# A hybrid mLSTM and sliding-window layer on one core: an account of PSUM banks for the interleaved chains, matrix-memory scores after their exponentials, and an out-projection norm in two operations

## The chip, the cores and the metric

The kernel runs on one core of a Trainium2 chip. The core has a matmul engine (TensorE, in the profile PE, with its weight loads shown apart as PEld), a vector engine (VectorE, DVE), an activation engine (ScalarE, ACT), a general engine (GpSimd, POOL) and an engine that issues most of the DMA transfers (SyncE, SP). Each engine works through its own queue of instructions in order; they wait for each other on semaphores. Matmul results land in PSUM, which this kernel uses as eight banks of 512 fp32 columns; everything else lies in SBUF.

The metric is the device time of one launch in microseconds (us). Lower is better.

## The reference, cut to what matters

One layer of a streaming encoder, on 2048 prompt rows (one sequence) and 128 sample rows (8 sequences of 16 rows with a cached state), each row 1024 wide, all in fp32:

```
z  = x @ w_in                       # q, k, v, output gate (4 heads x 128), two gates per head,
                                    # q (8 x 64), k and v (2 x 64) of the window attention
A: matrix memory, 4 heads, causal:  s = (q k^T) * exp(dmat - mt)
   num = w_inter * (q C) + s v ;  den likewise ;  h = num / max(|den|, exp(-mt))
   C' = decay * C + (wk * k)^T v    # state carried from chunk to chunk
   hm = sigmoid(o) * head_norm(h)
B: window attention: softmax over own and two earlier chunks of 64 rows, with a learned sink;
   mx = max(max(s), sink) ;  p = exp(s - mx) / (sum + exp(sink - mx))
mix = concat(hm, ha) @ w_out
h   = layer_norm(alpha * x + mix)   # the norm of the out-projection: g, b of 1024
u = h @ w_up ; causal conv of width 3 ; silu(gate) * value ; @ w_down
y   = layer_norm(alpha * h + f)
```

The outputs are y, the states of the matrix memory, the last keys and values, and the last rows of the convolution.

## The kernel before, in words

Rows are handled in 17 tiles of 128: 16 of the prompt and one (number 16) of all samples. Large products are made in three fp32r products of a high and a low half (`split` makes the halves: ACT casts, line 207, DVE subtracts, line 208), and many of them by a scheme of seven products for a 2 x 2 block.

The work runs in stages. First the in-projection (`i_dense`): four blocks of four tiles (the first has the sample tile too), and in each block five groups of columns with seven products each, and between blocks the narrow product of gates, keys and values (`i_direct`, `i_keys`). Then the out-projection (`o_block`): blocks of 3, 4, 4, 4 and 2 tiles. Then the up-projection, and then the down-projection.

The two token-mixing parts are chains of small steps, one tile after another: `m_chain` for the matrix memory, `a_chain` for the window attention, `t_sample` for the sample tile. They are written as generators, and their matmuls are placed by hand between those of the in-projection and the out-projection: PE's queue has the order in which the program writes it. The order on the other engines is made by the framework's scheduler.

The class `Chains` decides the place. It keeps a clock of its own, `t`. Each stretch of dense matmuls adds its cost to the clock (645 for 6 matmuls of 256 columns). Each step of a chain yields two numbers: the cost of its matmuls, and how long it then has to wait. `weave` takes the next step of a chain as soon as the clock has passed that time. `until` and `drain` take steps without waiting, where the out-projection needs a tile that is not mixed yet.

A chain's matmuls write to five PSUM banks that they share (`bank`, pool `tps`); the other three hold the dense results. For a tile of the matrix memory, in order: the gate rows are turned (pgr, `gate_rows`, `m_rows`), repeated over partitions (pm), and their columns taken (pcol); then scores (pscore) and turned keys (pkt); then numerators (pnum, two banks) and the state's products (pcu, two banks), from which DVE makes the new state C (line 1195) and `m_norm` the normed rows; then their transposes (pht). For a tile of the window attention: turned queries and keys (pq, pk), twice two banks of scores (psc), transposes of the probabilities (ppt, line 1310), products with the values (ppo).

In `m_tile` the step after pm computes the scores, the turned keys and the exponentials on ACT; the next takes the weighted scores (sd), the weighted keys (kw) on DVE and the weighted queries (qk times wi) on POOL.

The out-projection adds each half of a tile's product to alpha times x (line 1567), and after the second half calls `norm`: statistics on DVE, an inverse root on POOL (line 1524), then ACT (line 1537), DVE (line 1538) and POOL (line 1539), one after another over 1024 columns, and SP stores the row tile to `zh` (line 1570). In the out-projection the mixed rows of the next block are loaded and split too (`x_pair`), half of the low parts on POOL (line 881).

A block's tiles may enter the chains when `i_done` is raised: a counter of items after the narrow products of the block's first two tiles. The logarithms of the gates (`logs_of`, `gate_logs`, ending at line 976) come some items before that.

Of the kernel before, what the change touches and what calls it, by code (L numbers as in the profile page):

```python
# [30 lines left out]
NEG = -1e30  # L31
RING = 3

WB = 4
# [119 lines left out]
class Chains:  # L154

    def __init__(self, p):
        self.t, self.hold = 0.0, False
        self.done = {"m": -1, "a": -1, "s": False}  # L160
        self.p = p
        p.chains = self
        self.live = [[p.t_sample(), 0.0], [p.m_chain(), 0.0], [p.a_chain(), 0.0]]

    def step(self, c):
        r = next(c[0], None)
        if r is None:
            self.live.remove(c)
            return
        self.t += r[0]  # L170
        c[1] = self.t + r[1]

    def weave(self, dense):
        for cost in dense:
            self.t += cost
            if self.hold:
                continue
            for c in list(self.live):
                if c[1] <= self.t:
                    self.step(c)  # L180
# [14 lines left out]
class Prog:  # L195
# [377 lines left out]
    def i_dense(self):  # L573
        nc, a = self.nc, self.a
# [32 lines left out]
        after = None  # L607
        for item in self.items:
            if after:

                after[0] -= 1
                if after[0] == 1:
                    self.logs_of(after[1] - 1)
                if after[0] < 0:
                    self.i_done = after[1]
                    after = None
            self.chains.hold = item[0] == "t" and item[1] > 0
            if item[0] == "t":
# [8 lines left out]
                if ti == 1:  # L627
                    if b + 1 < nb:
                        self.x_steps(b + 1, 1, 2)
                    else:  # L630
                        self.release(4)
                    after = [4, b + 1]
                elif ti == 3 and b or ti == 4:
# [82 lines left out]
    def i_keys(self, b, ti, ps):  # L716
        nc = self.nc
        t = IBLOCKS[b][ti]
        kv = self.mp.tile([P, 2 * P], F32, name="kve", tag="kve", bufs=2)
        nc.scalar.copy(kv, ps[:, 8:264])  # L720
        nc.scalar.copy(self.gates[b][:, ti, :], ps[:, :8])
        self.rope(kv[:, :P], t, 1, nc.vector, self.zev())
        nc.sync.dma_start(self.zkv[t], kv)
# [115 lines left out]

    def rope(self, A, t, nt, adder, B=None):  # L840

        V = self.nc.vector
        n = A.shape[-1]
        if B is None:
            B = self.mp.tile([P, 512], F32, name="rb", tag="rb", bufs=1)
        B = B[:, :n]
        r, i0 = self.angles[t]
# [16 lines left out]
    def zev(self):  # L864
        return self.mp.tile([P, 512], F32, name="zev", tag="zev", bufs=6)

# [43 lines left out]

    def bank(self, shape, name):
        return self.tps.tile(shape, F32, name=name, tag="tb")

    def t_setup(self):
# [12 lines left out]
        self.sinkx = ld("sinkx")  # L927
        self.m0 = ld("m0")
        self.gm = ld("gm")
        nc.vector.tensor_scalar_mul(self.gm, self.gm, 0.5)  # L930
# [93 lines left out]
    def m_chain(self):  # L1024
# [4 lines left out]
        for t in range(NPT):  # L1029
# [3 lines left out]
            if pend is None:  # L1033
                pend = self.m_load(t, b, ti), *self.m_rows(t, b, ti)
                yield 300, 7000
            else:
                yield 0, 1000
            hn = self.m_norm(*(yield from self.m_tile(t, *pend)))
            pend = None
            yield 950, 3000  # L1040
            self.m_scaled(hn)
            if t + 1 < NPT and self.i_done > self.place(t + 1)[0]:
                pend = self.m_load(t + 1, *self.place(t + 1)), *self.m_rows(t + 1, *self.place(t + 1))
            yield 300, 9000
            self.m_out(t, hn[0])
# [114 lines left out]
    def m_tile(self, t, load, i, mp):  # L1160
# [6 lines left out]
        yield 600, 3000  # L1167
        emt = self.m_emt(col)
        ps = self.m_scores(qk)
        kt = self.m_ktok(qk)  # L1170
        wi = self.m_inter(pm, col)
        self.m_exps(dt, col)
        nc.gpsimd.tensor_mul(qk[:, 0:4], qk[:, 0:4], wi)
        yield 950, 6000
        sd = self.m_weighted(ps, dt)
        kw = self.work("kw", [P, MH, P])
        V.tensor_mul(kw, kt, dt[:, :, P - 1:P].to_broadcast([P, MH, P]))
        yield 0, 2500
        num = []
# [63 lines left out]
    def swa(self, t):  # L1243
        nc = self.nc
        V = nc.vector
        if self.a_first is None:
            self.swa_first(t)
            yield 550, 4000
        qh, ql = self.a_first
# [13 lines left out]
        def scores(kvh):  # L1263
            rs = slice(64 * kvh, 64 * kvh + 64)
            sink = self.sink[:, 4 * kvh:4 * kvh + 4]
            sc = self.work("sc", [P, 4, 2 * P], bufs=2)
            mx, es, sm = [self.work(n, [P, 4], bufs=2) for n in ("amx", "aes", "asm")]
            for j0 in (0, 2):
# [3 lines left out]
                for j in range(2):  # L1272
                    V.tensor_tensor_reduce(out=sc[:, j0 + j, :N], in0=ps[:, j, :nk].rearrange("p a b -> p (a b)"), in1=mask, scale=1.0, scalar=-3e38,
                                           op0=ALU.add, op1=ALU.max, accum_out=mx[:, j0 + j:j0 + j + 1])
            V.scalar_tensor_tensor(mx, mx, 0.125, sink, op0=ALU.mult, op1=ALU.max)
            V.tensor_sub(es, sink, mx)
            V.tensor_scalar_mul(mx, mx, -1.0)
            return sc, mx, es, sm
# [11 lines left out]
        z = [scores(0)]  # L1290
        yield 1300, 3000
        exps(*z[0])
# [8 lines left out]
        scs = [x[0] for x in z]  # L1301
        yield 0, 4000

        po = pts = None
        for kt in range(nk + 1):
# [221 lines left out]
    def norm(self, y, g, bb):  # L1527
        for _ in self.norm_steps(y, g, bb):
            pass

# [556 lines left out]
```

## Time and profile before

| | us |
|---|---|
| median of 3 runs | 2447.51 |
| the three runs | 2447.31, 2447.51, 2457.33 |
| the profiled execution, its own time | 2444.13 |
| its span in the profile | 2442.3 |

| stage (us from the start) | what runs |
|---|---|
| 0 to 700 | in-projection, with the sample tile's chain and the prompt tiles' chains 0 to 10 woven in |
| 700 to 960 | out-projection, with the rest of the chains |
| 960 to 2442 | last out-projection blocks, up-projection, down-projection |

The page of the profile gives each engine's busy time as a share of the span (PE 97%, DVE 76%, ACT 51%, POOL 15%), and the granted clock of the matmul engine, 0.988 on average. The list of waits says which instruction waited, for whom, for how long in total, how often and how long at most. The windows give each engine's busy time in a stretch, and the clock in it. A timeline row has the start, the duration, the engine, the line, the operation, what it writes and reads, how many instructions are merged into it and, in brackets, how long the engine was idle before and what ended that.

### The profile page before, as it was taken

To read this page: it belongs to the slowest core of one execution; us is meant where nothing else is said; L and a number is where in the kernel's file an instruction comes from. 1 tells how busy PE (TensorE), PEld (TensorE's weight loads), DVE (VectorE), ACT (ScalarE), POOL (GpSimd) and SP (SyncE) were. 2 spreads that over 40 slices of the span, in tenths; PEclk is the share of its full clock that TensorE was granted. 3 is DMA by queue.
4 is the path that set the end of the run, shared out by engine and by line. 5 is a ranking of instruction groups with operands and counts; after the bars stand their busy time and mean duration, and the time that the engine had idled before them with its cause. 6 is when DMAs were issued, how large, how long until landed. Compare 5 with 4: busy or idle time off the path is not lost.

```text
span 2442.3 us, 39931 instructions
## 1 busy us (share of the span) xinstructions
PE 2357.2 (97%) x14425; PEld 2159.0 (88%) x14425; DVE 1853.2 (76%) x3211; ACT 1252.7 (51%) x2310; POOL 359.1 (15%) x369
## 2 busy tenths in 40 slices
PE   8989999999998899999999999999999999999998
PEld 8989988988987677799999999999999978778776
DVE  8677487686687776997788776778766777896897
ACT  5443365565554553655555555445544544444543
POOL 0101102212224333200000000002000100210400
PEclk9999999999998999999999999999999999999999
DMA  8898988778794446587777889887998776756653
GB/s 292 299 306 308 312 287 300 252 241 298 244 314 150 151 153 230 197 318 289 282 267 269 279 308 324 303 282 243 315 295 260 248 270 212 234 179 216 212 189 104
DMA packets 296933, 624.98 MB, mean 256 GB/s; under 512 B 47004, under 2 KB 140192, under 8 KB 296736
## 3 DMA queue, kind: packets, MB, share of 16 engines
q1 hardware_dynamic: 294144, 612.99, 74.3%
q0 software_dynamic: 1728, 6.29, 0.7%
q10 hardware_dynamic: 864, 3.15, 0.4%
q8 instruction: 114, 1.87, 0.3%
q14 instruction: 83, 0.68, 0.1%
HBM read 451.78 MB, written 170.56 MB: 255 GB/s over the span
## 4 chain that ended last, share of the span: by engine, by line
PE 68%; DVE 11%; DMA 8%; issue 4%; ACT 3%; POOL 1%; SPq 0%; DVEq 0%; ACTq 0%; POOLq 0%
PE fup L1790 15%; PE dps L1790 15%; PE dps L686 10%; PE fht L1993 5%; PE dps L1993 5%; PE fup L1993 3%; DMA zf<-cc 2%; DVE w L208 2%; PE dps L212 2%; PE dps L213 1%; PE dps L214 1%; DVE cc L1838 1%; DVE uw L208 1%; PE ppo L1316 1%; PE ppt L1310 1%
## 5 line engine op out<-in xcount | busy, mean ns | idle before, releaser
L1790 PE MATMUL dps<-hh,uw 128*128 128x384 f32 (+1 forms) x1848 | 481.8, 329 | 8.6 <-ACT u L1815 3.7
L1790 PE MATMUL fup<-hh,uw 128*128 128x384 f32 (+1 forms) x1848 | 481.1, 329 | 3.7 <-ACT u L1815 2.4
L1790 PEld LDWEIGHTS dps<-hh,uw 128*128 128x128 f32 x1848 | 330.2, 188 | 12.4 <-ACT u L1815 4.8
L1838 DVE SCALAR_TENSOR_TENSOR cc<-u,cw,cc 128x768 f32<-128x768 f32 (+1 forms) x264 | 252.5, 978 | 111.3 <-ACT cc L1836 109.3
L1790 PEld LDWEIGHTS fup<-hh,uw 128*128 128x128 f32 x1848 | 330.4, 188 | 5.5 <-ACT u L1815 3.5
L1790 PE MATMUL fup<-hl,uw 128*128 128x384 f32 (+1 forms) x924 | 303.2, 328 | 2.9 <-DVE hl L208 2.9
L1790 PE MATMUL dps<-hl,uw 128*128 128x384 f32 (+1 forms) x924 | 302.8, 328 | 0.0
L686 PE MATMUL dps<-w,oh 128*128 128x256 f32 x1344 | 260.0, 288 | 3.8 <-ACT zev L753 1.4
L208 DVE TENSOR_TENSOR w<-wraw,w 128x1024 fp32r<-128x1024 f32 (+2 forms) x167 | 204.1, 1230 | 68.0 <-ACT w L207 65.8
L207 ACT CAST w<-wraw 128x1024 fp32r<-128x1024 f32 (+2 forms) x167 | 162.8, 983 | 162.0 <-PE dps L686 74.1
L686 PEld LDWEIGHTS dps<-w,oh 128*128 128x128 f32 x1344 | 214.1, 191 | 17.6 <-issue 8.1
L207 ACT CAST uw<-wraw 128x1024 fp32r<-128x1024 f32 x126 | 122.9, 978 | 202.6 <-PE dps L1993 94.1
L208 DVE TENSOR_TENSOR uw<-wraw,uw 128x1024 fp32r<-128x1024 f32 x126 | 150.9, 1199 | 61.7 <-ACT uw L207 61.5
L1836 ACT ACTIVATE cc<-u,cw 128x768 f32<-128x768 f32 (+1 forms) x132 | 129.6, 998 | 124.4 <-DVE u L1829 60.8
L686 PE MATMUL dps<-oh,w 128*128 128x256 f32 x896 | 175.3, 290 | 16.8 <-ACT dps L781 5.9
L686 PE MATMUL dps<-w,ol 128*128 128x256 f32 x672 | 189.7, 282 | 0.0
L1993 PE MATMUL fup<-uw,fu 128*128 128x512 f32 x726 | 176.4, 399 | 8.9 <-DVE yacc L2022 4.5
L1790 PEld LDWEIGHTS fup<-hl,uw 128*128 128x128 f32 x924 | 173.8, 188 | 3.5 <-DVE hl L208 3.5
L1993 PEld LDWEIGHTS fup<-uw,fu 128*128 128x128 f32 x726 | 137.2, 190 | 43.7 <-DVE yacc L2022 5.4
L1790 PEld LDWEIGHTS dps<-hl,uw 128*128 128x128 f32 x924 | 173.8, 188 | 0.0
L686 PEld LDWEIGHTS dps<-oh,w 128*128 128x128 f32 x896 | 145.4, 195 | 25.0 <-ACT dps L781 6.5
L1993 PE MATMUL dps<-uw,fu 128*128 128x512 f32 x660 | 164.7, 396 | 0.0
(331 smaller groups left out, 4818.4 us busy)
## 6 DMA issues: line engine op xcount, KB each, us to landing
uw<-zw SPq DMA_DIRECT2D x176, 512.0 KB, 4.9
zw<-uw SPq DMA_DIRECT2D x88, 512.0 KB, 2.9
w<-zws SPq DMA_DIRECT2D x72, 512.0 KB, 5.6
wv<-wup SPq DMA_DIRECT2D x66, 512.0 KB, 5.2
wraw<-wi SPq DMA_DIRECT2D x65, 512.0 KB, 5.0
wraw<-zt SPq DMA_DIRECT2D x60, 512.0 KB, 4.2
wraw<-wdn SPq DMA_DIRECT2D x45, 512.0 KB, 3.8
wraw<-wo SPq DMA_DIRECT2D x40, 512.0 KB, 4.3
```

The lines of the kernel that those rows point to most:

```text
L207: nc.scalar.copy(hi, src)
L208: nc.vector.tensor_sub(lo, src, hi.bitcast(F32))
L212: mm(out, ah, bh, start=start, stop=False)
L213: mm(out, ah, bl, start=False, stop=False)
L214: mm(out, al, bh, start=False, stop=stop)
L686: mm(o, l, r, start=s in (1, 7) and c == k == i == 0, stop=k == 3 and i == 2, skip_group_check=True)
L1310: nc.tensor.transpose(pp[:, j * P:(j + 1) * P], scs[kvh][:, j, kt * P:(kt + 1) * P], self.ident)
L1316: nc.tensor.matmul(po[64 * kvh:64 * kvh + 64], w, pts[:, kvh], start=kt == 1, stop=kt == nk)
L1790: mm(ps, l[:, k], r[:, k], start=s in (1, 7) and k == 0 and i == 0, stop=k == 3 and i == 2, skip_group_check=True)
L1836: S.activation(c[:, v], u[:, v, 2:2 + n], AF.Identity, bias=w[3], scale=w[2])
L1838: V.scalar_tensor_tensor(c[:, v], u[:, v, i:i + n], w[i], c[:, v], op0=ALU.mult, op1=ALU.add)
L1993: mm(ps, l[:, k, c], r[:, k], start=s in (1, 4, 7) and u == 0 and k == 0 and i == 0, stop=u == nu - 1 and k == n - 1 and i == 2, skip_grou ...
```

## The change

The clock of the chains also keeps a list of five times, one for each bank of the chains' pool. Each call of `bank` drops the oldest entry and appends the present time plus a hold that depends on the bank's name (6500, 4000, 5000, 6500, or 3500 for the others). A step may yield a third number, the banks that the next step will ask for; `weave` takes that step only when so many of the oldest entries have passed.

In `m_tile` the exponentials and the weights `wi` come in a step of their own; scores and turned keys follow 5000 later, together with the weighted scores, keys and queries. Some waiting times of the chains are other numbers.

The norm of the out-projection becomes two DVE operations of full width: (y - mean) * g, and then y * (inverse deviation) + b.

Apart from these: the negated sink is made once, and the negated maximum of the scores comes from one operation and not from two; the counter before `i_done` goes from 4 to 6, the logarithms stay at the same item; evicted keys and values take a slot of the ring `zev` (now seven slots, before six) in place of their own tiles, and their rotation uses the scratch tile `rb`.

```diff
+NBANKS = 5
+HOLDS = {"pm": 6500, "pgr": 4000, "pnum": 5000, "ppo": 6500}
 class Chains:
-        self.live = [[p.t_sample(), 0.0], [p.m_chain(), 0.0], [p.a_chain(), 0.0]]
+        self.live = [[p.t_sample(), 0.0, 0], [p.m_chain(), 0.0, 0], [p.a_chain(), 0.0, 0]]
+        self.free = [0.0] * NBANKS
     def step(self, c):
...
         c[1] = self.t + r[1]
+        c[2] = r[2] if len(r) > 2 else 0
+
+    def ask(self, hold):
+        self.free = self.free[1:] + [self.t + hold]
     def weave(self, dense):
...
-                if c[1] <= self.t:
+                if c[1] <= self.t and max(self.free[:c[2]], default=0) <= self.t:
                     self.step(c)
     def i_dense(self):
...
-                if after[0] == 1:
+                if after[0] == 3:
                     self.logs_of(after[1] - 1)
...
-                    after = [4, b + 1]
+                    after = [6, b + 1]
     def i_keys(self, b, ti, ps):
-        kv = self.mp.tile([P, 2 * P], F32, name="kve", tag="kve", bufs=2)
+        kv = self.zev()[:, :2 * P]
         nc.scalar.copy(kv, ps[:, 8:264])
...
-        self.rope(kv[:, :P], t, 1, nc.vector, self.zev())
+        self.rope(kv[:, :P], t, 1, nc.vector)
     def rope(self, A, t, nt, adder):
-        if B is None:
-            B = self.mp.tile([P, 512], F32, name="rb", tag="rb", bufs=1)
-        B = B[:, :n]
+        B = self.mp.tile([P, 512], F32, name="rb", tag="rb", bufs=1)[:, :n]
     def zev(self):
-        return self.mp.tile([P, 512], F32, name="zev", tag="zev", bufs=6)
+        return self.mp.tile([P, 512], F32, name="zev", tag="zev", bufs=7)
     def bank(self, shape, name):
+        self.chains.ask(HOLDS.get(name, 3500))
         return self.tps.tile(shape, F32, name=name, tag="tb")
     def t_setup(self):
+        self.nsink = self.one("nsink", [P, 8])
+        nc.vector.tensor_scalar_mul(self.nsink, self.sink, -1.0)
     def m_chain(self):
-                yield 300, 7000
+                yield 300, 7000, 2
             else:
-                yield 0, 1000
+                yield 0, 1000, 2
...
-            yield 950, 3000
+            yield 950, 3000, 1
             self.m_scaled(hn)
...
-            yield 300, 9000
+            yield 300, 7500, 1
             self.m_out(t, hn[0])
     def m_tile(self, t, load, i, mp):
         yield 600, 3000
         emt = self.m_emt(col)
+        wi = self.m_inter(pm, col)
+        self.m_exps(dt, col)
+        yield 0, 5000, 2
         ps = self.m_scores(qk)
         kt = self.m_ktok(qk)
-        wi = self.m_inter(pm, col)
-        self.m_exps(dt, col)
-        nc.gpsimd.tensor_mul(qk[:, 0:4], qk[:, 0:4], wi)
-        yield 950, 6000
         sd = self.m_weighted(ps, dt)
         kw = self.work("kw", [P, MH, P])
         V.tensor_mul(kw, kt, dt[:, :, P - 1:P].to_broadcast([P, MH, P]))
-        yield 0, 2500
+        nc.gpsimd.tensor_mul(qk[:, 0:4], qk[:, 0:4], wi)
+        yield 950, 3500, 4
     def a_chain / swa(self, t):
-            yield 550, 4000
+            yield 550, 4000, 2
...
-            V.scalar_tensor_tensor(mx, mx, 0.125, sink, op0=ALU.mult, op1=ALU.max)
-            V.tensor_sub(es, sink, mx)
-            V.tensor_scalar_mul(mx, mx, -1.0)
+            V.scalar_tensor_tensor(mx, mx, -0.125, sink[1], op0=ALU.mult, op1=ALU.min)
+            V.tensor_add(es, sink[0], mx)
...
-        yield 1300, 3000
+        yield 1300, 3000, 2
...
-        yield 0, 4000
+        yield 0, 3500, 2 + 2 * (self.a_load is not None)
...
-            yield (860 if kt < nk else 0) + (1400 if kt else 0), 0 if kt == nk else 1500 if kt else 3000
+            yield (860 if kt < nk else 0) + (1400 if kt else 0), 0 if kt == nk else 1500 if kt else 3000, 2 * (kt + 1 < nk) + (kt == 0)
     def norm(self, y, g, bb):
-        for _ in self.norm_steps(y, g, bb):
-            pass
+        V = self.nc.vector
+        mv, s = self.stats(y)
+        V.scalar_tensor_tensor(y, y, mv[:, 0:1], g, op0=ALU.subtract, op1=ALU.mult)
+        V.scalar_tensor_tensor(y, y, s[:, 0:1], bb, op0=ALU.mult, op1=ALU.add)
```

More of the change, by code (lines that the diff above doesn't have):

```diff
@@ L838, in d_sums, with rope @@
         nc.sync.dma_start(self.zt[1, k], y)
-    def rope(self, A, t, nt, adder, B=None):
+    def rope(self, A, t, nt, adder):
         V = self.nc.vector
         n = A.shape[-1]
-        if B is None:
-            B = self.mp.tile([P, 512], F32, name="rb", tag="rb", bufs=1)
-        B = B[:, :n]
+        B = self.mp.tile([P, 512], F32, name="rb", tag="rb", bufs=1)[:, :n]
         r, i0 = self.angles[t]
@@ L1264, in scores @@
             rs = slice(64 * kvh, 64 * kvh + 64)
-            sink = self.sink[:, 4 * kvh:4 * kvh + 4]
+            sink = [x[:, 4 * kvh:4 * kvh + 4] for x in (self.sink, self.nsink)]
             sc = self.work("sc", [P, 4, 2 * P], bufs=2)
```

## The prediction, made before the changed kernel ran

> **What bounds the kernel now.** I read the page first (busy shares), then the waits of the matmul engine alone, then windows by stage, then the vector and GpSimd timelines around the longest waits.
>
> ```profile
> PE 2357.2 (97%) x14425; PEld 2159.0 (88%) x14425; DVE 1853.2 (76%) x3211; ACT 1252.7 (51%) x2310; POOL 359.1 (15%) x369
> ```
>
> The matmul engine (PE) is busy 97% of the span, and the change leaves the number and shapes of its matmuls as they are (13961 in both written orders). So the change can only win PE's idle time, and the slow stretches that follow it. The waits of PE from 160 to 1000 us, where the chains and the out-projection run (total, times, longest):
>
> ```profile
> PE ppt L1310 <- DVE C L1195: 13.4, 4, 5.1
> PE dps L686 <- ACT dps L781: 6.7, 4, 4.3
> PE dps L686 <- ACT gates L721: 4.8, 4, 2.4
> PE pgr L985 <- DVE g L976: 4.0, 1, 4.0
> PE dps L213 <- DVE w L208: 2.3, 1, 2.3
> PE pm L1079 <- DVE hl L993: 2.1, 1, 2.1
> ...
> PE ppo L1316 <- ACT pth L1311: 1.5, 1, 1.5
> ```
>
> All rows of that answer sum to 40.6 us: the ceiling of idle time. The windows by stage, and short windows just behind four waits (length, PE, PEld, DVE, ACT, POOL busy, granted clock):
>
> ```profile
> 160.00:700.00 540.00, 521.06 (x4144) 484.93 (x4144) 385.28 (x1050) 288.83 (x713) 98.61 (x74) 0.98 0.85 282
> 700.00:960.00 260.00, 240.14 (x1227) 189.60 (x1226) 191.69 (x498) 125.70 (x304) 91.61 (x56) 0.95 0.58 192
> ...
> 755.30:761.90 6.60, 4.66 (x16) 4.12 (x17) 5.59 (x24) 2.40 (x7) 0.00 (x0) 0.50 0.93 290
> 779.20:785.80 6.60, 6.60 (x25) 5.80 (x25) 3.08 (x18) 6.34 (x27) 1.90 (x1) 0.50 0.72 206
> ...
> 913.00:921.00 8.00, 4.83 (x27) 2.51 (x25) 6.89 (x22) 1.92 (x5) 6.53 (x3) 1.00 0.80 260
> ```
>
> The out-projection (700 to 960) loses most: 20 us idle, and a clock of 0.95. Behind a wait the clock can stand at 0.50 for 3.3 or 6.6 us, so half of what PE works there is lost too: 4.66/2 = 2.3 us behind the 5.0 us wait at 752.
>
> Why the vector engine (DVE) released that bank so late, DVE and POOL around 750 us:
>
> ```profile
> 745.91 3.42 DVE L881 TENSOR_TENSOR ol<-xraw,oh 128x1024 fp32r<-128x1024 f32 x1
> 749.26 6.65 DVE L208 TENSOR_TENSOR w<-wraw,w 128x1024 fp32r<-128x1024 f32 x2
> ...
> 756.51 1.10 DVE L1195 SCALAR_TENSOR_TENSOR C<-C,wi,pcu 128x129 f32<-128x129 f32 x4
> ```
>
> ```profile
> 744.94 3.31 POOL L1539 TENSOR_TENSOR ymix<-ymix,o_ln_b 128x1024 f32<-128x1024 f32 x1 [1.16 <-PE dps L214]
> 748.21 6.63 POOL L881 TENSOR_TENSOR ol<-xraw,oh 128x1024 fp32r<-128x1024 f32 x2
> ```
>
> A DVE split that takes 1.22 us elsewhere takes 3.4 beside the POOL sum of the norm (L1539) and 3.3 beside POOL's splits: they run one after the other. The norm's own rows (min/median/max in ns), and the form that the change uses, at half width (L1595):
>
> ```profile
> L1537 ACT ACTIVATE ymix<-ymix,lsc x15: 1224/1242/1247, 741.7 to 986.1; 128x1024 f32<-128x1024 f32 x15
> L1538 DVE TENSOR_TENSOR ymix<-ymix,o_ln_g x15: 1214/1226/3046, 742.9 to 987.9; 128x1024 f32<-128x1024 f32 x15
> L1539 POOL TENSOR_TENSOR ymix<-ymix,o_ln_b x15: 2347/2410/3413, 744.9 to 991.1; 128x1024 f32<-128x1024 f32 x15
> ...
> L1595 DVE SCALAR_TENSOR_TENSOR ymix<-ymix,lmv,lnp x4: 742/746/747, 1046.7 to 1073.4; 128x512 f32<-128x512 f32 x4
> ```
>
> **The change part by part.**
>
> (a) Account of banks. In the order before, 8 of 16 tiles have no projection matmul between the state products (pcu) and the probability transposes (ppt) that take their banks. In the new order every tile has 36 of 256 columns or 18 of 512 there: 36 x 0.118 or 18 x 0.233 (start to start) = 4.2 us. The three long ppt waits (5.02, 5.05, 3.17) lack 5.0, 5.1 and 3.2 us; 4.2 more, with an earlier DVE by (c), covers them. Gain 13.2, and the half clock behind two of them, 2.3 + 2.4. Sum -17.9; bounds 0 (DVE later by as much) and -17.9.
>
> (b) Tiles of a block start two products later (counter 6 for 4) while the gate logarithms stay at the third item. The wait pgr <- g of 4.0 us ended at 183.5; two products are 48 x 0.118 = 5.7 us, so it goes, with 5.0/2 = 2.5 of half clock (181.8 to 188.5, PE busy 5.0). -6.5. The later start costs nothing while the chains end in time: in neither order is a step taken out of its pacing to feed an out-projection block. Without that cover it would be 3 x 5.7.
>
> (c) Norm. Per tile one ACT operation of 1.24 and one POOL sum of 2.41 go, and a small DVE operation of 0.16. On DVE 1.23 becomes two of full width: 746 ns for 512, and 1.02 for 768 in L1838, so some 1.29 for 1024, an estimate from these rows. 15 x (2.58 - 1.23 - 0.16) = +18 us of DVE, against 15 POOL sums (36 us at their median) that no longer hold up DVE's two-input operations by up to 2.2 us each (3.42 against 1.22). Net on DVE between -15 and +18; I take 0, as DVE (74% here) hides either.
> The norm's result comes earlier: today statistics at 933.8, the last store at 943.4 after ACT, DVE, POOL in turn; two DVE operations for two tiles need 4 x 1.29, ending at 939. That store's landing (951.6) held ACT's queue: a load of rows for the next stage waits there, with the weight casts behind it (ACT idle 9 us until 952.05), and PE waited 0.7 for ACT's w and 2.3 for DVE's, then 3.3 at half clock. 4.4 us earlier removes it: -3.0 - 1.65 = -4.7; bounds 0 and -4.7. pm <- hl (2.1, then 6.6 at half clock) stood behind scans stretched to 2.60 and 1.99 by the POOL sum, but four new operations (5.2) now queue in DVE just ahead of it: half of 5.4, -2.7; bounds 0 and -5.4. ppo <- pth (1.5): half, -0.7.
>
> The page "SBUF — State Buffer" of the Trainium skill ("Who interferes with whom") says a vector instruction with two SBUF inputs and a GpSimd one that reads SBUF exclude each other, first come first. The 3.42 above agrees. By it the new operations queue against POOL's 12 divisions here (1.89 each) as well, up to 23 us more of DVE; if a fifth of that reached PE the sum would be -21.
>
> (d) Scores behind their exponentials. pscore, pkt, DVE's sd and kw and POOL's query multiply (1.34) move later; no DMA moves. Between the key transposes and pnum lay 36 to 156 matmuls (mostly 42 to 84); now always 36 of 256 or 18 of 512, 4.2 us, and 5.1 for kw. In most tiles of today's trace sd and kw end 1.5 to 2 us after pkt, so nothing waits. In two they would: sd at 708.1 with pkt ended at 701.7 (late by 2.2), kw at 515.1 after 508.2 (1.8). About +4, and half clock behind one, +3: +7; bounds 0 and +25 (rival 1 begins there).
>
> (e) Maximum negated at once: 32 operations of 0.16 go, 5 us of DVE spread wide; 0. Its bounds are 0 and -4.3, the one wait on dps L781, which ACT's exponentials delayed while L1277 took 1.87.
>
> (f) Keys in a zev slot instead of kve, rotation scratch in rb: the slot is held until its store lands (4.0 us at 519.6), hidden by the seventh slot; without that cover ACT's copies wait, bounded by today's zev waits of 0.9. The one rb is shared with POOL's sums: 0.
>
> Sum: -17.9 - 6.5 - 4.7 - 2.7 - 0.7 + 7 = -25.5. The profiled execution took 2444.1, the median of three 2447.5 (two at 2447.3 and 2447.5), 3.4 above. 2444.1 - 25.5 = 2418.6, and as the median may stand 0 to 3.4 above its profile I say 2421.
>
> "TensorE: Matmul & The Clock Gate" of the Trainium skill (Part 1) has the half clock only after an idle window of about 3.4 us. By it the 1.65 and half of 3.3 for shorter waits fall away, sum -22. The trace differs: 2.1 us idle was followed by 6.6 us at 0.50, 3.2 idle (at 914) by 1.00.
>
> **Rivals.**
> 1. Slower: the query multiply stands behind a division. In the new POOL order 11 of 16 tiles have a division of probabilities (1.89) ahead of the multiply (1.34). In the in-projection pnum comes some 8.0 us after the start of the second score product (12 score matmuls, 12 projection matmuls and 8 of keys, 3.8 us, then 4.2); the multiply must start by 6.6. Today's divisions end 2.4 to 2.9 after that product in smooth tiles, but 5.5 to 10.7 in the out-projection. If each tile were late by 1.2, idle and half clock cost 16 x (1.2 + 1.65) = 46: 2444 - 25 + 46, about 2465. It decides from 2.3 us per tile, idle and half clock together (37 = the gain of 25 and 12 more). Against it: the smooth tiles' 3.7 us of margin.
> 2. Same: the wait moves. DVE, not the order, is late; the next thing PE asks of it (pm, pnum) waits instead. Then (b) and a little of (c) remain: -7, 2440. For it: DVE 74% busy in bursts; against it: (c) frees POOL.
> 3. The banks stay as they were: the written order excludes it.
>
> **Chances.** Forecast 0.64; rival 2 0.22; rival 1, or DVE with +18 exposed, 0.14. A difference of 0.5% (12 us) is about what a measurement tells from none. Faster 0.64, same 0.22, slower 0.14. Range: 2404 (every gain in full, (e) too, no new wait: -40) to 2444 (rival 2 with nothing kept); the forecast alone 2404 to 2432.
>
> **What would show it.** Right: no ppt <- C above 1 us, no pgr <- g, clock of 700 to 960 at 0.98 or more, L208's mean there below 1.4. Wrong: waits of pnum on sd or qk, or of pm on hl, that sum to over 15 us.

## The result, and the profile after

The changed kernel takes 2419.1 us (median of 4 runs, 2416.1 to 2426.5) against 2447.5 before. The ratio is 0.988, with a 95% interval of 0.985 to 0.991. The forecast was 2421 with a range of 2404 to 2444: sign, size and range held. The sum behind it did not hold as well, as the experiments show.

The profiled execution took 2419.2 us with a span of 2417.4, against 2444.1 and 2442.3 before, so the two profiles differ by 24.9 us. The busy shares of the changed kernel, the first view of the page:

```profile
PE 2353.0 (97%) x14425; PEld 2156.0 (89%) x14425; DVE 1844.3 (76%) x3180; ACT 1235.4 (51%) x2295; POOL 328.8 (14%) x354
```

PE has as many instructions as before (14425).

PE's waits from 160 to 1000 us (total, times, longest), the answer to the list in the prediction:

```profile
PE dps L696 <- DMA w<-zws: 6.7, 6, 3.2
PE pq L1223 <- DMA qa<-zqa: 3.4, 1, 3.4
PE dps L223 <- DVE w L218: 3.1, 1, 3.1
PE ppt L1321 <- POOL sc L1299: 2.7, 1, 2.7
PE ppt L1321 <- DVE C L1206: 2.3, 2, 1.3
PE pm L1090 <- DVE hl L1004: 2.3, 1, 2.3
...
PE ppo L1327 <- ACT pth L1322: 1.4, 1, 1.4
...
PE pgr L996 <- DVE g L987: 0.3, 1, 0.3
...
PE pnum L1195 <- DVE sd L1118: 0.2, 1, 0.2
```

Four rows of the old list are gone, wholly or nearly: 11 of the 13.4 us of ppt on C, all 6.7 of dps on ACT's dps (line 781), 3.7 of the 4.0 of pgr on g, and all 4.8 of dps on gates (a row that the prediction quoted and gave no price). Others came or grew: dps on w<-zws from 0.7 to 6.7, ppt on POOL's sc from nothing to 2.7, pq on qa<-zqa from 1.1 to 3.4, dps on ACT's zev from 0.9 to 2.6. Two stayed where the prediction had them go or shrink: the wait on DVE's w, now at 933, and pm on hl.

The windows by stage, and one behind the wait at 247 (length, PE, PEld, DVE, ACT, POOL busy, granted clock, DMA share, GB/s):

```profile
160.00:700.00 540.00, 522.33 (x4163) 487.03 (x4161) 387.77 (x1034) 287.01 (x704) 100.45 (x74) 0.98 0.84 283
700.00:960.00 260.00, 251.64 (x1302) 198.50 (x1302) 198.37 (x505) 120.17 (x309) 71.75 (x47) 0.98 0.61 205
...
249.80:256.40 6.60, 5.61 (x24) 5.34 (x25) 0.89 (x2) 1.14 (x4) 0.76 (x1) 0.50 1.04 403
```

The norm's two operations, the rows that take the place of ACT's, DVE's and POOL's (min, median and max in ns):

```profile
L1541 DVE SCALAR_TENSOR_TENSOR ymix<-ymix,lmv,o_ln_g x15: 1273/1275/1279, 736.8 to 965.1; 128x1024 f32<-128x1024 f32 x15
L1542 DVE SCALAR_TENSOR_TENSOR ymix<-ymix,lsc,o_ln_b x15: 1265/1277/3409, 738.6 to 967.5; 128x1024 f32<-128x1024 f32 x15
```

In the out-projection PE is busy 251.6 of 260 us (240.1 before) at a clock of 0.98 (0.95 before). The in-projection gained almost nothing: 522.3 for 521.1 at the same clock. Counting dense matmuls says the same (those that write dps, psx, pg or fup; the counts below are of these). The 1500th starts 12.9 us earlier than before (in part because 24 matmuls of the sample's chain now come behind it), the 1950th at the same time (292.5 for 292.4), the 4050th, where the out-projection begins, 0.8 us earlier, the 4950th, behind the out-projection, 23.0 us earlier.

Two numbers per trace explain almost the whole span of every kernel below. One is PE's listed waits between 160 and 1000 us. The other is the length of the stretches there in which the granted clock stood at 0.50; half of that is counted as lost.

| kernel | waits, us | at 0.50, us | waits + half | span |
|---|---|---|---|---|
| before | 40.6 | 44.4 | 62.8 | 2442.3 |
| changed | 27.6 | 30.7 | 42.9 | 2417.4 |
| changed, old norm | 34.9 | 47.8 | 58.8 | 2439.5 |
| changed, counter 4 | 21.7 | 10.2 | 26.8 | 2400.4 |
| changed, no account | 28.3 | 44.4 | 50.5 | 2429.4 |
| changed, counter 4, no account | 28.2 | 27.3 | 41.9 | 2421.5 |

Span less the fourth column lies between 2373.6 and 2380.7 for these six, and between 2371.6 and 2380.8 for all fourteen profiles. The spans themselves lie 44 us apart.

### The profile page after: what moved, and what is told of

Its sections match the earlier page's. It is cut to its first block, busy times and chain, and to the rows that moved or that the text cites. A ratio compares the mean times of both kernels' runs of the same rounds, so it can differ in the third digit from the quotient of the medians.

```text
span 2417.4 us, 39808 instructions
## 1 busy us (share of the span) xinstructions
PE 2353.0 (97%) x14425; PEld 2156.0 (89%) x14425; DVE 1844.3 (76%) x3180; ACT 1235.4 (51%) x2295; POOL 328.8 (14%) x354
## 4 chain that ended last, share of the span: by engine, by line
PE 77%; DVE 9%; DMA 6%; issue 4%; ACT 2%; POOL 1%; SPq 0%; DVEq 0%; POOLq 0%; ACTq 0%
PE dps L1803 17%; PE fup L1803 17%; PE dps L696 12%; PE fht L2006 5%; PE dps L2006 5%; PE fup L2006 4%; PE dps L222 2%; PE dps L223 2%; PE dps L224 2%; PE dps L722 2%; PE ppo L1327 1%; DVE w L218 1%; DMA w<-zws 1%; DVE uw L218 1%; PE ppt L1321 1%
## 5 line engine op out<-in xcount | busy, mean ns | idle before, releaser
L1803 PEld LDWEIGHTS dps<-hh,uw 128*128 128x128 f32 x1848 | 329.9, 188 | 10.2 <-ACT u L1828 2.4
L218 DVE TENSOR_TENSOR w<-wraw,w 128x1024 fp32r<-128x1024 f32 (+2 forms) x167 | 199.1, 1202 | 55.8 <-ACT w L217 50.5
L218 DVE TENSOR_TENSOR uw<-wraw,uw 128x1024 fp32r<-128x1024 f32 x126 | 150.7, 1197 | 61.1 <-ACT uw L217 60.9
```

Of the source, the lines that this page charges most:

```text
L218: nc.vector.tensor_sub(lo, src, hi.bitcast(F32))
L1803: mm(ps, l[:, k], r[:, k], start=s in (1, 7) and k == 0 and i == 0, stop=k == 3 and i == 2, skip_group_check=True)
```

## The experiments

Each ratio is against runs of the kernel before on the same chip; 0.01 is 24.5 us. Ratios are what is compared, since the kernel before had medians of 2447.5 to 2453.0 in these comparisons. Differences of two ratios carry both intervals, added in quadrature.

| run | edit | median, us | ratio (95%) |
|---|---|---|---|
| changed kernel | | 2419.1 | 0.9879 (0.9846 to 0.9912) |
| u_norm | old norm back | 2437.3 | 0.9940 (0.9921 to 0.9959) |
| u_normv | old norm, last sum on DVE | 2423.0 | 0.9883 (0.9861 to 0.9905) |
| b_norm | before + new norm | 2434.8 | 0.9918 (0.9895 to 0.9941) |
| u_banks | no account | 2429.2 | 0.9906 (0.9884 to 0.9929) |
| c4_banks | counter 4, no account | 2423.9 | 0.9896 (0.9878 to 0.9914) |
| u_order | scores ahead of exponentials | 2424.0 | 0.9891 (0.9863 to 0.9919) |
| u_count | counter 4 | 2407.1 | 0.9824 (0.9800 to 0.9847) |
| log3 | counter 4, logarithms earlier | 2407.1 | 0.9816 (0.9793 to 0.9839) |
| c8 | counter 8 | 2416.9 | 0.9864 (0.9845 to 0.9884) |
| late_st | state stored a step later | 2417.8 | 0.9866 (0.9844 to 0.9889) |
| c4_x | counter 4, splits on DVE | 2403.6 | 0.9816 (0.9795 to 0.9837) |
| c4_xd | counter 4, splits and divisions on DVE | 2399.4 | 0.9794 (0.9776 to 0.9812) |

### The norm: undone, alone, and without its POOL sum

```
u_norm, in norm() of the changed kernel:
-        V = self.nc.vector
-        mv, s = self.stats(y)
-        V.scalar_tensor_tensor(y, y, mv[:, 0:1], g, op0=ALU.subtract, op1=ALU.mult)
-        V.scalar_tensor_tensor(y, y, s[:, 0:1], bb, op0=ALU.mult, op1=ALU.add)
+        for _ in self.norm_steps(y, g, bb):
+            pass
u_normv: the same, but self.norm_steps(y, g, bb, self.nc.vector)
b_norm: the kernel before, with the new four lines of norm() alone
```

> The changed kernel (2419.1) with the old norm of the out-projection put back (one scaling on ACT, the product on DVE, the sum on POOL); the order of the matmuls stays as in the changed kernel. By the sum of the prediction the norm is worth 4.7 + 2.7 + 0.7 = 8 us, so about 2427; waits of ppt on C stay below 3 us in all, as the order of the matmuls covers them. Rival, the norm carries the out-projection: DVE is held up by POOL's sums as before, and a distance of 4.2 us does not cover a release that is 3 to 5 us late; then ppt on C comes back between 700 and 960 with 5 us or more, the clock there falls to 0.96 or less, and the time is 2433 to 2440. As the wait at the end of the out-projection (933) is there with the new norm too, the 4.7 of the sum may be worth nothing: then 2422.

> The changed kernel with the old norm, but with its last sum on DVE in place of POOL: ACT's operation of 1.24 us and the small one stay, DVE has the same two wide operations as with the new norm, POOL has none. If POOL's sums cost by holding up DVE's two-input operations, the 18 us of the old norm are gone: 2419 to 2424. If the old norm costs by its way through three engines (ACT in the middle, DVE waiting for it in order, 7.5 us of such waits between 700 and 960 before), most of the 18 stay: 2431 to 2437, with the waits of pm on hl and of ppo that the old norm brought.

> The kernel before with the new norm alone; banks, counters and the order in a tile stay as they were (8 of 16 tiles with nothing between pcu and ppt). By the sum of the prediction (4.7 + 2.7 + 0.7) it gains 8 us: 2439, and the 13 us of ppt on C stay. If the norm is worth as much here as it is in the changed kernel, where putting the old one back cost 18, it gains 18: 2429; and if POOL's sums were what released the banks late, ppt on C between 700 and 960 falls from 13.3 to below 6. If the two parts overlap (each alone cures the same waits), it gains more than 18, since the account was worth only 10 on top of the new norm.

Putting the old norm back costs 0.0061, 15 us (plus or minus 9). Moving only its sum from POOL to DVE recovers 0.0057, 14 us (plus or minus 7). On the kernel before, the new norm alone gains 0.0082, 20 us (plus or minus 6). The prediction had 8.1 for the norm, which the last of these excludes. So the sum's engine makes nearly the whole difference, and no cost of ACT's place in the old norm can be told (1 us, plus or minus 10).

How it costs is seen at one tile. DVE and then POOL in the kernel with the old norm, around 768 us:

```profile
766.15 2.34 DVE L1549 TENSOR_TENSOR ymix<-ymix,o_ln_g 128x1024 f32<-128x1024 f32 x2
768.42 2.36 DVE L1003 CAST hl<-r_M 4x128 fp32r<-4x128 f32 x1
770.81 2.33 DVE L1007 SCALAR_TENSOR_TENSOR ay<-r_b,r_M 4x128 f32<-4x128 f32 x1
773.07 0.27 DVE L1004 TENSOR_TENSOR hl<-r_M,hl 4x128 fp32r<-4x128 f32 x1
```

```profile
767.43 5.56 POOL L1550 TENSOR_TENSOR ymix<-ymix,o_ln_b 128x1024 f32<-128x1024 f32 x2 [2.57 <-DVE ymix L1549]
```

The same operations with the sum on DVE:

```profile
762.01 2.36 DVE L1550 TENSOR_TENSOR ymix<-ymix,o_ln_b 128x1024 f32<-128x1024 f32 x2
764.28 0.21 DVE L1003 CAST hl<-r_M 4x128 fp32r<-4x128 f32 x1
764.52 0.28 DVE L1007 SCALAR_TENSOR_TENSOR ay<-r_b,r_M 4x128 f32<-4x128 f32 x1
764.73 0.28 DVE L1004 TENSOR_TENSOR hl<-r_M,hl 4x128 fp32r<-4x128 f32 x1
```

A cast of 4 x 128 elements that takes 0.21 us takes 2.36 beside POOL's two sums, and the operation after it 2.33 for 0.28. So the row of gates that PE waits for comes over 4 us late. The Trainium skill ("SBUF — State Buffer", "Who interferes with whom") has casts among the operations that can, where their operands allow it, take the port pair shared with GpSimd, and then one side blocks fully; these rows agree. The largest waits of the out-projection with the old norm in the changed kernel (700 to 960):

```profile
PE pm L1090 <- DVE hl L1004: 4.5, 1, 4.5
PE dps L223 <- DVE w L218: 3.6, 1, 3.6
PE ppo L1327 <- DVE ay L1067: 3.2, 1, 3.2
PE pnum L1195 <- DVE sd L1118: 2.1, 1, 2.1
PE ppt L1321 <- DVE C L1206: 2.0, 1, 2.0
```

The loss is not in one wait. Whatever PE asks of DVE next is late. The rival's figure (2433 to 2440) was met, but not its place: ppt on C has 2.0, not the 5 or more that it expected, and the clock of the stage is 0.97.

In the kernel before with the new norm alone, the same stage:

```profile
PE ppt L1310 <- DVE C L1195: 8.9, 3, 3.6
PE dps L213 <- DVE w L208: 4.7, 1, 4.7
```

Of 13.3 us of ppt on C, 8.9 stay, and the longest falls from 5.1 to 3.6. With the distance and the old norm it was 2.0 above, so for this wait the distance does more than the norm, as far as single profiles tell. The profiled execution of this run is the slowest of its six (2441.8), so the gain is read from the times.

### The account of banks

```
u_banks, in weave() of the changed kernel:
-                if c[1] <= self.t and max(self.free[:c[2]], default=0) <= self.t:
+                if c[1] <= self.t:
c4_banks: the same, on the kernel with counter 4
```

> The changed kernel without the account of banks: a step is taken as soon as its time has come, whatever the banks (the steps' own numbers, the order inside a tile and the new norm stay). In this order 13 of 16 tiles have no projection matmul between pcu and ppt (8 in the kernel before, none in the changed one). By the prediction the account is worth 17.9 us: 2437, with ppt on C waiting 13 us or more in all. Rival, the new norm alone cured it: DVE releases in time even without the distance, ppt on C stays below 4 us, and the time is 2419 to 2424. Nothing else of the chains waits longer in either case.

> The run with counter 4 without the account of banks: 13 of 16 tiles have nothing between pcu and ppt. With counter 6 the account was worth 10 us by the medians (ratio 0.9906 for 0.9879, intervals that overlap). If that is the account's worth and not that of one alignment, it shows here as well: 2414 to 2420, and ppt on C waits 8 us or more in all. If the worth comes only from where the tiles happen to fall, it is within 4 of 2407.

With counter 6 the account is worth 0.0027, 7 us (plus or minus 10): not told from nothing, and the time (2429.2) lies between the two readings of the expectation. Yet without it the wait that it was made against is back, in many short pieces, half of it (5.1 us) in the out-projection:

```profile
PE ppt L1321 <- DVE C L1206: 10.2, 7, 2.3
```

With counter 4 the account is worth 0.0072, 18 us (plus or minus 7), the 17.9 of the forecast. But it does not lie where the forecast had it. PE's waits from 160 to 1000 us with counter 4 and no account:

```profile
PE dps L696 <- ACT dps L791: 6.4, 4, 3.5
...
PE ppt L1321 <- DVE C L1206: 2.6, 5, 0.9
```

Ppt on C is only 2.6 us, against the 8 that were expected (and 0.7 with the account). Against counter 4 with the account, the 4050th dense matmul already starts 19.1 us later, and the whole out-projection adds 2. Of the 19.1 some 5 are 39 matmuls of the chains that now come before the out-projection and not in it (an estimate at the 0.131 us that one takes there on average). Summed over start-to-start times from 160 us up to the 4950th dense matmul, PE spends 6.7 us more behind ppt, 5.3 behind pkt, 2.0 behind pht and 1.7 behind pq, the chains' transposes. The rest is in the projections. With counter 6, where the same stretches hold as many matmuls with the account as without, 9.9 us more pass from the 1950th to the 4050th without it (426.9 for 417.0), and 1.3 more from there to the 4950th. So the account's worth is mostly in small stalls of the in-projection, where chain steps come close together, and in half clock (27.3 us at 0.50 for 10.2 with counter 4). That closeness makes these stalls is argued; no run moved single steps.

### The start of the sample tile: counter 4, 6, 8

```
u_count: - after = [6, b + 1]   + after = [4, b + 1];   - if after[0] == 3:   + if after[0] == 1:
c8:      - after = [6, b + 1]   + after = [8, b + 1];   - if after[0] == 3:   + if after[0] == 5:
log3:    - after = [6, b + 1]   + after = [4, b + 1]
```

In the written order the counter moves the first block alone: setting it back to 4 for that block only gives the same instructions on every engine, since the later blocks' tiles are not waiting for it. But the shift is carried on: PE's order with 4 and with 6 differs from 177 us until some 900 us, through most of the out-projection. With 8 it is that of 6 again from 506 us on.

> The changed kernel with the tiles of a block started two products earlier again (counter 4, the gate logarithms at its last item). By the prediction 6.5 us slower: 2425.5, pgr on g waiting 4 us again near 180. Rival, what the later start won there was given back in the in-projection, through the loads of the sample tokens that then meet the weight loads between 240 and 320 (dps on w<-zws 6.7 us in all, and half clock behind it): then pgr on g comes back, these waits go, and the time is 2417 to 2421.

> The changed kernel with the sample tile started two products earlier (counter 4, as in the kernel before) and the gate logarithms two items earlier than there (at the first item after the gates, not at the third). The orders of the other tiles are those of the run with counter 4 (2407). Pgr on g waits 5.8 us in that run, and half clock follows; the logarithms two items earlier start some 5 us earlier. If that wait is the logarithms' late start, it falls below 1.5 and the time is 2400 to 2403. Rival: DVE has the rotation of the keys to do just then, the logarithms push it back and the wait moves to the projection's own tiles (dps on zev), so 2405 to 2409.

> The changed kernel with the sample tile started two products later still (counter 8, the gate logarithms at the third item as before): the step of the change from 4 to 6, taken a second time. With 4 the time was 2407, with 6 it was 2419, though pgr on g waits 5.8 us with 4 and 0.3 with 6. If the later start costs because the sample's loads and stores then fall among the loads of kept weights (w<-zws, two of 512 KB for a product), the cost grows: w<-zws waits 8 us or more in all and the time is 2424 to 2432. If 6 was only one unlucky alignment (the stalls at 247, 764 and 933), another start falls otherwise: 2407 to 2417, with w<-zws below 4. If the wait on g is worth what the sum said and 6 took it all, 8 changes nothing there: 2417 to 2421.

This is the step where the prediction had the sign wrong. Counter 4 is 0.0055 faster than 6, 13 us (plus or minus 10). Its twin with earlier logarithms is 0.0063 faster, and against counter 8 the two are 0.0040 and 0.0048 faster. The wait that the later start was to remove is real. PE's waits with counter 4, 160 to 1000 us:

```profile
PE pgr L996 <- DVE g L987: 5.8, 1, 5.8
PE dps L696 <- ACT dps L791: 4.2, 3, 2.6
PE pnum L1195 <- DVE sd L1118: 2.1, 2, 1.9
...
PE dps L696 <- DMA w<-zws: 0.2, 1, 0.2
```

The later start is 8.8 us ahead at the 1500th dense matmul (202.3 for 211.1), 3.6 of it only because 24 matmuls of the sample's chain now come later. By the 1950th it is behind (292.5 for 287.5). What takes it back is the stretch between them, where the weights that were kept in DRAM come back: 90.2 us for 76.4, with 4.2 more for the chain, 6.3 more of listed waits (7.4 for 1.1) and 6.8 more at half clock. This is no accident of one execution: PE's waits there are 6.4 to 7.4 us in the six profiles with counter 6, 4.7 with counter 8, and 1.1 to 2.3 in the seven with counter 4 (two of them with the order of the kernel before). SP's queue in the changed kernel:

```profile
226.85 0.33 SPq L451 DMA_DIRECT2D wraw<-wi  x1
233.22 0.37 SPq L741 DMA_DIRECT2D zqk<-zev  x1
233.68 0.91 SPq L479 DMA_DIRECT2D w<-zws  x2
238.63 0.34 SPq L1423 DMA_DIRECT2D cn_s<-cns  x1
...
242.65 0.33 SPq L451 DMA_DIRECT2D wraw<-wi  x1
243.03 0.42 SPq L1443 DMA_DIRECT2D kvc<-kcT  x1
243.50 0.42 SPq L1444 DMA_DIRECT2D kvc<-vc  x1
244.03 0.85 SPq L479 DMA_DIRECT2D w<-zws  x2
```

SP stands three times for 3 to 6 us at a store or load that is not ready. The weights of the next product are issued behind that, right after the sample's cache, and PE stands at them for 3.2 us at 247, with 6.8 us at half clock behind. With counter 4 the first cache load went out at 221.5. With counter 8 w<-zws waits 4.7 in all, the longest 3.3. The cost did not grow with another two products, so the first reading in the expectation for 8 falls, and neither of the others fits whole. So the later start meets loads there, and that the harm hangs on which transfers fall together is argued, not shown.

One attempt to name the transfer:

```
late_st:
-                nc.sync.dma_start(a["cn_s"][:, h], cn)
                 vws = weighted(h + 1) if h + 1 < MH else None
                 yield 4000, 3500
+                nc.sync.dma_start(a["cn_s"][:, h], cn)
```

> The changed kernel (counter 6), with one thing moved: the sample tile's store of a head's state is issued one step later, when DVE has long written it. The order of the matmuls is untouched. In the changed kernel SP's queue stands at that store for 4.0 us (234.6 to 238.6) and at others behind it, and the weight loads w<-zws that PE waits for (6.7 us, the longest 3.2 at 246.9) are queued behind. If the order of SP's queue is what gave back the gain of the later start, these waits fall below 3 and the time is 2408 to 2414. If the sample's transfers and the weight loads collide on the DMA engines themselves (0.96 busy there), the waits stay and the time is 2417 to 2421.

The waits stay (w<-zws 8.3 in all), as does the time (0.9866 for 0.9879). But the queue was hardly freed: SP still stood 2.5 us at a store of the state (4.0 before) and then until 241.2 at the next raw weights, and the kept weights were issued at 242.6 in place of 244.0. So this does not decide between the queue's order and the transfers themselves. That the store alone is not the cause is seen better with counter 4, where SP stands at it just as long (7.1 us in two places between 222 and 262, 7.6 with counter 6) and w<-zws waits 0.2. The cause in this stretch stays open.

The rest of the 13 us lies in the out-projection. From the 4050th to the 4950th dense matmul the changed kernel takes 300.0 us, with counter 4 it takes 290.3; with as many chain matmuls in it (610), the four profiles with counter 4 and the account take 288 to 291, and the four with 6 or 8, the new norm and the new order in a tile take 299 to 302. With 4 PE's waits between 700 and 960 sum to 2.8 us and the clock is 1.00. With 6 and with 8, whose order there is the same, the same two stalls appear, pm on hl at about 763 and DVE's w at about 934. Here is the latter in the changed kernel, first DVE, then SP:

```profile
922.04 0.67 DVE L1580 SCALAR_TENSOR_TENSOR ymix<-ymix,dps 128x512 f32<-128x512 f32 x1
...
934.63 0.69 DVE L1580 SCALAR_TENSOR_TENSOR ymix<-ymix,dps 128x512 f32<-128x512 f32 x1 [9.17 <-DMA ymix<-x]
935.24 1.22 DVE L218 TENSOR_TENSOR w<-wraw,w 128x1024 fp32r<-128x1024 f32 x1
```

```profile
921.31 0.33 SPq L1583 DMA_DIRECT2D zh<-ymix  x1
923.08 0.33 SPq L1571 DMA_DIRECT2D ymix<-x  x1
923.50 0.45 SPq L1583 DMA_DIRECT2D zh<-ymix  x1
929.61 4.27 SPq L1571 DMA_DIRECT2D ymix<-x  x2
```

DVE stands 9.2 us at an addition whose rows are still being loaded, and the splits of weights are queued behind it. That load could be issued only at 929.6, when the store of 921.3 had freed the slot. Between 910 and 930 the DMA share is 1.01, with the next stage's rows among the loads. So the shorter norm did not spare the wait for its store to land, on which the prediction had put 4.7 us.

The run with earlier logarithms hardly moved them. They begin on DVE at 168.5 and end at 180.3; with counter 4 alone they begin at 167.9 and end at 180.6. In both their 17 small operations take turns in DVE's queue with splits of 1.22 us, and some 12 us pass from the first to the last. So whether an earlier start would help was not tested. The wait is 4.9 for 5.8, and the time is unchanged; the rival's time came, but not its wait (dps on zev is 0.5).

### Scores ahead of their exponentials

```
u_order, in m_tile() of the changed kernel: scores, key transposes, then wi, exps and the query multiply;
yield 950, 6000; sd, kw; yield 0, 2500, 4 (the lines of the kernel before, with the counts of banks)
```

> The changed kernel with scores and key transposes ahead of the exponentials again, 8.4 us of projection matmuls between the key transposes and pnum in place of 4.2 (the account of banks stays). By the prediction the new order costs 7 us in waits of pnum, so 2412. Rival, from the trace of the changed kernel, where pnum waits 0.2 in all: the order costs nothing, and 2419 within 3. Second rival: the scores' banks are asked for earlier and held longer, so a later step (ppt, ppo) has to wait for a bank or is pushed back; then 2422 or more with waits of ppt on C or of pq.

The ratio differs by 0.0012 (plus or minus 0.0043). No effect can be told. The cost of 7 us that was forecast (a ratio near 0.985) lies at the very edge of the interval, and the profile of the changed kernel does not have it: 0.2 us of pnum on sd where the forecast had 4. With the old order ppt on C waits 1.6, so the second rival has no sign either.

### More of POOL's work on DVE

```
c4_x:  - (nc.gpsimd if b < nb - 1 and p % 2 else nc.vector).tensor_sub(l, raw, h.bitcast(F32))
       + nc.vector.tensor_sub(l, raw, h.bitcast(F32))
c4_xd: that, and - nc.gpsimd.tensor_mul(sc[:, :, :N], ...   + V.tensor_mul(sc[:, :, :N], ...
```

> The run with counter 4 (2407, ratio 0.982) with one thing more: the 8 residual splits of the out-projection's input that go to POOL (2.41 us each) go to DVE. Where a DVE operation with two inputs and a wide POOL operation exclude each other, 8 x 2.41 us of POOL become 8 x 1.22 on DVE, and DVE is held up 9.5 us less: 2400 to 2406, and the splits of weights (L218) between 700 and 960 have a mean below 1.25. Rival: DVE only gets 10 us more to do in a stage where it is 80% busy, and the time stays or grows: 2407 to 2413.

> As the run before, and the 32 divisions of probabilities on DVE too (on POOL 1.94 us each). By the same exclusion 62 us of POOL become 39 us of DVE (1.22 each), and the wait of ppt on POOL's sc goes with them: 2396 to 2404. Rival: the divisions now stand in DVE's queue between rotations and splits, which were free to run beside the narrower work; DVE goes from 75% to 80% busy in the in-projection, and what waits for it there (dps on zev, pnum on sd) loses more than the exclusion costs: 2410 to 2420.

The splits of weights between 700 and 960 with counter 4, and with all eight splits and 32 divisions off POOL (min, median and max in ns):

```profile
L218 DVE TENSOR_TENSOR w<-wraw,w x36: 1196/1220/3324, 703.0 to 959.0; 128x1024 fp32r<-128x1024 f32 x36
```

```profile
L218 DVE TENSOR_TENSOR w<-wraw,w x36: 1198/1220/1227, 702.1 to 956.3; 128x1024 fp32r<-128x1024 f32 x36
```

The split stretched to 3.3 us is gone. DVE's busy time between 700 and 960 grows only from 208.6 to 218.4 us while POOL's falls from 73.8 to 35.0. The splits alone cannot be told from no change (0.9816 for 0.9824). With the divisions it is 0.9794, 7 us (plus or minus 7) better than counter 4, which is at the edge of what can be told, 21 (plus or minus 9) better than the changed kernel and 50 better than the kernel before. It has the lowest median here.

## Why the prediction was right, and where it was not

**(a) Account, -17.9.** The size is borne out with counter 4 (18) and left open with 6 (7, plus or minus 10). The mechanism was right for the named wait and missed the rest. The distance of 4.2 us does shorten ppt on C, from 10.2 to 2.3 with counter 6, and the norm alone does less (8.9 of 13.3 left in the order of the kernel before). Most of the account's worth with counter 4 is in the in-projection, on which the sum had put nothing. That its size came out at 17.9 is luck.

**(b) Later start, -6.5.** The step that failed. The wait went as said (0.3 left). "The later start costs nothing while the chains end in time" was wrong. The counter shifts what meets between the 1500th and the 1950th dense matmul (7.4 us of waits for 1.1) and the order of PE through the out-projection (300.0 us for 290.3), and together this costs 13 us more than it gave. The cover that the prediction named, no forced steps, was true and beside the point.

**(c) Norm, -8.1.** The mis-sized term: 15 to 20. The operation's price was right (1.275 and 1.277 us for the 1.29 estimated). The net on DVE was set at 0 between -15 and +18 because DVE "hides either", and the gain was looked for in named waits. It came from everything that POOL's sums held up, the smallest operations most in proportion (0.21 to 2.36). Of the two waits that it did name, neither went: pm on hl is 2.3 for 2.1 (with 3.4 us of half clock behind for 6.6), and DVE's w is 3.1 at 933 for 2.3 (and 0.7 on ACT's) at 952, with 6.8 us of half clock behind for 3.4. Ppo on pth is 1.4 for 1.5.

**(d) Order in the tile, +7.** No cost can be told (3 us the other way, plus or minus 11). Pnum waits 0.2 us in the changed kernel and 2.9 with counter 4.

**(e) Negated maximum, 0.** Not run by itself. The wait on dps L781 that bounded it is absent from the changed kernel's list, but 4.2 us with counter 4, so it is not the negation that decides it.

**(f) Keys in a zev slot, 0.** The row that was missed. The keys' copies before, who they wait for and who waits for them:

```profile
L720 ACT COPY kve<-dps x14: 348/372/389, 160.4 to 700.5; 128x256 f32<-128x256 f32 x14
...
  DMA zkv<-kve: 9.5, 3
```

ACT stood 9.5 us in three places until a store of keys had landed and freed one of two kve slots; the copies of gates stand behind these, and PE had 4.8 us of dps on gates. That row is in the kernel before and with the new norm alone (4.0), and in none of the kernels with the seventh zev slot. The change of slots was not run by itself, so its 4 to 5 us are read from traces; against them stand 1.7 us more on zev, which the sum had bounded by 0.9 in all.

**Rivals.** The first (query multiply behind a division) did not come: no such wait in the changed kernel, 0.8 us with counter 4. The second (the wait moves) described the out-projection with the old norm better than the kernel that was run. That the banks stay as they were did not happen.

**The sum.** Forecast: -17.9 - 6.5 - 8.1 + 7 = -25.5. By the runs with counter 4, everything else in the change is worth 43 us (1 - 0.9824), and the counter takes about 13 back. The parts as measured (18, 15 to 20, 4 to 5) come to 37 to 43, though not all in the same kernel. That the total was met is luck: a gain too small, a row without a price and a cost that did not come made up for a term of the wrong sign.

Of the signs set down in advance, pgr on g, the clock of 0.98 and L218 (mean 1.26 for 1.52) came as said. Ppt on C above 1 us remains twice (1.3 and 1.1).

## What to carry to other kernels

Price an operation on GpSimd by what it holds up on VectorE, down to the smallest cast, and not by whether it is on the path: moving a sum to an engine that was 76% busy made the kernel faster. A step that is started later gets a new set of neighbours in every queue and every later stage, so a wait removed at its start has to be followed to the end of the last stage before it is counted. Go through the list of waits row by row and ask of each edit which row it touches; the row that nobody priced was one of the four that went.

## What the runs showed that was not expected

The half clock costs a good part of what the waits cost: 44.4 us at 0.50, counted as 22 lost, beside 40.6 us of waits before, 5 lost beside 21.7 with counter 4, 26 beside 25.5 in the run with the later store. All 87 stretches in the fourteen profiles last 3.4 us or two, three or four times that. What brings one on is not the length of one wait. A single wait of 5.8 us (counter 4, at 175) was followed by 3.4 us at 0.50, one of 3.1 (changed kernel, 933) by 6.8, one of 2.3 (764) by 3.4. "TensorE: Matmul & The Clock Gate" of the Trainium skill (Part 1) sets the gate by idle windows of about 3.4 us that run freely; the lengths of 3.4 and 6.8 agree with that, half clock after 2.3 us of listed wait does not agree with a whole idle window.

Some stretches follow no wait at all. With counter 4 two of the three, at 268.7 and 296.0, begin just as the sample tile's window attention ends a run of 32 matmuls of 64 columns, and PE is busy without a gap before (length, PE, PEld, DVE, ACT, POOL busy, granted clock, DMA share, GB/s):

```profile
265.30:268.70 3.40, 3.40 (x29) 2.52 (x28) 0.00 (x0) 1.31 (x2) 0.00 (x0) 0.99 0.98 337
268.70:272.10 3.40, 3.40 (x17) 3.17 (x17) 1.64 (x2) 0.00 (x0) 0.00 (x0) 0.50 0.68 229
```

These matmuls start 0.13 us apart, no closer than those of 256 columns (0.118). Twenty of the 87 stretches come so, one or two in nearly every profile, and no list of waits shows them.

The same instructions on PE do not keep the same pace from one execution to the next in the in-projection. In the kernel before and in the one with the new norm alone it is the same code, and its 4050th dense matmul starts at 710.3 and at 719.8. Differences below 10 us in that stage can't be read from one trace.
